# A two-layer attention trunk whose instructions are issued in another written-out order

## The chip, the cores and the metric

The kernel runs on one core of one Trainium2 chip. The metric is the device time of one execution, in microseconds (us). The kernel before took 305.75 us, the median of three runs from 305.56 to 307.73 us. One further execution was taken with the hardware profiler; it took 305.27 us, and 303.5 us of it are the span that the profile shows.

## The reference, cut to what matters

One sequence of 256 tokens with 1024 channels goes through two layers. Each layer computes a shift, a scale and a gate from a condition vector `c`, normalises `x`, projects it, attends and adds the gated result to `x`:

```
cond = silu(c)
for i in range(2):
    shift, scale, gate = split(cond @ ada_w[i] + ada_b[i], 3)
    h = rms_norm(x, norm_g[i]) * (1 + scale) + shift
    y = nsa_mixer(h, ...) if i == 0 else moba_mixer(h, ...)
    x = x + gate * y
```

The first mixer projects `h` to queries, keys and values of three kinds (compressed, selected, window), gates and an output gate `z`. Queries and keys get an RMS norm and a rotation by tables of sines and cosines from the positions. The compressed keys and values go through a small two-layer network. The second mixer is causal attention with 16 heads over 4 key heads. Each mixer ends with a product with an output matrix.

## The kernel before, in words

All weights are read from memory as float32 and split into a high part (rounded to the fast format) and a low part (the rest). Each product is three matmuls: high by high, low by high and high by low. ScalarE makes the high part with a copy, VectorE the low part with a subtraction (`products_of`, lines 1067 and 1068, for the first projection; `parts_of` for later ones).

**The order is written out by hand.** The kernel does not issue instructions where its code stands. It records them as numbered operations with their dependences (`Plan.record`), and at the end `Plan.issue` goes through the list `ORDER`, 2403 numbers, and issues the operations one after the other. Since almost all instructions are issued by one line of `Plan.issue`, they all have line 302 in the profile; groups are told apart by the names of their tiles. The list sets three things. Each engine (TensorE, ScalarE, VectorE, GpSimd and SyncE, which issues most transfers) takes its operations in the order of the list, and waits where an operand isn't ready. A tile gets its buffer when its first operation is issued, from those that earlier tiles have given back. And the transfers get their completion semaphores in that order.

**The opening.** SyncE loads the two halves of `x` (operations 1 and 2) and the weights, stage by stage. ScalarE's queue issues three small transfers: `c` (0), `norm_g` (3) and `ada_b` (4), into the tiles `rot` and `y`. GpSimd's queue issues eight: the norm weights and the gate bias (6 to 10, one row tile `y`), two for the compression (11 and 12, tile `rot`) and the positions (5, tile `rs`). The first projection is done for eight slices of 128 channels, k = 0 to 7. For a slice, four transfers bring the piece of `ada_w` for shift and scale (tile `early`, 41 to 44 for k = 0, 48 to 51 for k = 1), three bring the weight rows (45 to 47 for k = 0). TensorE then runs these steps before the first projection matmul (102):

- 18 to 37: twenty matmuls on an identity that only keep the engine busy.
- 16: transpose of `c`; VectorE and ScalarE make the gated condition `condz` from it (17, 38 to 40).
- 72, 74, 78, 80: transposes of the normalised `x`, four to a group; ScalarE copies the results into `xT` (73, 75, 79, 81).
- 85 and 86 (k = 0), 122 and 123 (k = 1): the condition times `ada_w`, eight calls each, into one row; VectorE copies the row (87, 124).
- 88, 125: a matmul with a selector (`selP`) that turns the row into columns.
- 82: transpose of `norm_g` and `ada_b` into columns (`RT`, 83 and 84). VectorE makes the affine pair `AB` from the columns and 88 (89, 90).
- 91 to 93: ScalarE and VectorE write the slice of `h`, the tile `HT`, high and low part, for k = 0.
- 222, 226, 293: small matmuls that spread the norm weights over all partitions, transpose the positions, and transpose the compression rows.

GpSimd then computes the rotation tables from the positions (228 on). After the eight slices come the key norm and rotation, the compression network, the queries, the blocks of `z`, two pairs of attention heads and the output product, and then the second layer in the same way. While the attention of the first layer runs, side work (the other parts of `ada_w`) is put between.

Of the kernel before, what the change touches and what calls it, by code (L numbers as in the profile page):

```python
# [37 lines left out]
    0, 48, 41, 1, 2, 42, 45, 43, 44, 50, 18, 19, 20, 21, 22, 23, 24, 16, 25, 26, 27, 28, 29, 30, 31, 32, 52, 17, 38,  # L38
    3, 39, 54, 55, 40, 56, 53, 4, 62, 63, 57, 64, 58, 65, 59, 33, 85, 34, 35, 36, 37, 60, 66, 61, 67, 70, 12, 5, 8,
    10, 9, 11, 6, 7, 68, 69, 71, 72, 86, 87, 74, 76, 88, 82, 78, 77, 49, 51, 47, 46, 122, 80, 123, 83, 84, 90, 89,  # L40
    225, 226, 94, 73, 75, 91, 108, 81, 95, 102, 103, 99, 105, 106, 100, 164, 132, 133, 177, 165, 131, 175, 162, 163,
    323, 176, 324, 219, 206, 207, 209, 208, 221, 220, 124, 227, 92, 93, 110, 101, 116, 125, 222, 109, 117, 126, 224,
    127, 223, 79, 128, 148, 104, 118, 107, 113, 114, 111, 115, 112, 119, 150, 120, 121, 293, 156, 153, 134, 129,
    149, 130, 135, 13, 294, 96, 154, 157, 97, 139, 98, 151, 178, 136, 137, 166, 167, 326, 325, 179, 168, 192, 152,
    142, 169, 143, 170, 171, 14, 15, 172, 173, 193, 174, 331, 332, 144, 145, 146, 147, 189, 158, 140, 194, 159, 160,
    138, 161, 200, 201, 202, 186, 180, 181, 141, 203, 190, 191, 295, 296, 228, 271, 229, 230, 231, 232, 270, 272,
    278, 233, 234, 235, 236, 237, 238, 250, 239, 240, 241, 242, 243, 244, 245, 251, 246, 247, 248, 249, 263, 252,
    253, 254, 264, 265, 266, 284, 255, 273, 309, 210, 211, 155, 195, 212, 213, 183, 184, 197, 185, 198, 204, 215,
    214, 216, 187, 188, 306, 182, 205, 196, 303, 311, 300, 297, 310, 317, 298, 318, 333, 217, 334, 218, 329, 327,
    328, 330, 335, 336, 319, 320, 321, 322, 301, 304, 305, 312, 199, 302, 314, 307, 337, 338, 339, 313, 315, 316,  # L50
    299, 308, 349, 351, 350, 380, 411, 412, 381, 414, 382, 413, 416, 415, 418, 599, 417, 439, 437, 352, 366, 353,
    340, 342, 341, 367, 344, 343, 282, 256, 257, 258, 280, 259, 292, 275, 290, 260, 288, 261, 287, 274, 289, 281,
    262, 267, 279, 269, 268, 283, 286, 276, 285, 291, 277, 360, 374, 361, 354, 371, 375, 345, 376, 372, 373, 377,
    355, 368, 346, 383, 362, 391, 356, 369, 378, 397, 357, 370, 358, 419, 347, 420, 384, 402, 421, 422, 423, 348,
    359, 385, 399, 388, 379, 363, 364, 365, 394, 389, 392, 390, 405, 393, 395, 386, 387, 396, 424, 438, 469, 620,
    576, 577, 468, 470, 621, 598, 643, 580, 642, 794, 764, 749, 841, 440, 425, 426, 427, 398, 428, 429, 430, 406,
    403, 404, 407, 400, 408, 409, 410, 431, 445, 448, 442, 401, 441, 454, 432, 455, 433, 462, 449, 451, 443, 578,
    452, 586, 579, 450, 463, 464, 465, 466, 587, 588, 459, 446, 447, 434, 471, 476, 589, 479, 460, 444, 472, 435,
    461, 436, 467, 590, 456, 457, 458, 591, 473, 477, 485, 600, 478, 608, 490, 601, 486, 491, 492, 474, 480, 609,
    610, 453, 482, 481, 483, 644, 507, 510, 511, 622, 623, 592, 593, 594, 595, 596, 597, 614, 615, 616, 617, 618,  # L60
    619, 611, 612, 636, 613, 630, 631, 632, 633, 634, 637, 475, 638, 484, 645, 750, 751, 487, 639, 640, 641, 488,
    665, 635, 655, 656, 666, 667, 489, 668, 669, 670, 842, 508, 843, 509, 503, 765, 501, 502, 504, 500, 505, 506,
    844, 493, 657, 658, 659, 758, 494, 752, 845, 846, 753, 754, 847, 848, 849, 856, 495, 660, 857, 496, 759, 760,
    755, 497, 566, 858, 859, 766, 756, 761, 860, 762, 861, 763, 773, 757, 767, 768, 498, 774, 769, 770, 561, 771,
    520, 521, 672, 522, 779, 602, 871, 901, 512, 872, 874, 671, 780, 523, 524, 525, 662, 526, 527, 781, 673, 873,
    554, 677, 567, 528, 710, 513, 625, 581, 499, 661, 902, 663, 850, 556, 568, 529, 569, 530, 570, 565, 559, 678,
    795, 775, 571, 851, 852, 776, 777, 875, 720, 876, 877, 778, 772, 788, 878, 879, 886, 853, 887, 888, 789, 782,
    790, 572, 574, 903, 783, 854, 855, 889, 890, 791, 891, 792, 904, 905, 906, 862, 863, 793, 864, 865, 804, 796,
    558, 674, 562, 564, 557, 679, 518, 603, 515, 624, 582, 583, 584, 585, 604, 605, 606, 607, 907, 866, 784, 785,
    908, 909, 916, 805, 786, 917, 918, 806, 787, 807, 808, 919, 920, 867, 563, 680, 555, 575, 531, 560, 532, 533,  # L70
    681, 536, 682, 664, 676, 534, 535, 683, 684, 537, 685, 686, 675, 687, 573, 688, 689, 690, 691, 550, 546, 547,
    921, 551, 944, 945, 947, 647, 646, 519, 652, 626, 627, 628, 629, 648, 649, 650, 651, 693, 692, 694, 695, 552,
    553, 946, 538, 702, 548, 703, 549, 542, 543, 797, 708, 544, 696, 653, 869, 868, 709, 948, 949, 809, 798, 950,
    880, 799, 800, 951, 952, 959, 801, 881, 539, 882, 883, 802, 884, 885, 704, 711, 712, 713, 714, 810, 715, 540,
    803, 739, 545, 716, 697, 698, 717, 746, 744, 811, 718, 541, 719, 812, 654, 724, 699, 705, 721, 725, 813, 726,
    814, 727, 815, 728, 870, 899, 928, 516, 929, 1019, 898, 700, 706, 960, 961, 1008, 962, 963, 994, 988, 964, 707,
    816, 729, 817, 730, 818, 731, 819, 723, 722, 820, 732, 745, 747, 821, 733, 1009, 734, 735, 737, 822, 995, 823,
    989, 736, 824, 738, 900, 930, 748, 826, 825, 740, 1079, 517, 1074, 1077, 941, 942, 1010, 1011, 1020, 971, 997,
    992, 701, 991, 993, 996, 931, 990, 1002, 932, 935, 934, 933, 1073, 1076, 514, 1080, 827, 741, 998, 1012, 1124,
    892, 742, 1104, 893, 828, 1003, 835, 829, 999, 1007, 1005, 1001, 743, 1000, 1013, 1125, 972, 1006, 1014, 1105,  # L80
    1114, 1028, 975, 894, 1115, 1126, 1109, 1127, 895, 896, 897, 910, 911, 1021, 1029, 912, 1128, 913, 1030, 1117,
    1004, 1116, 1107, 1015, 1108, 976, 836, 977, 830, 1016, 978, 979, 1017, 936, 1106, 1018, 1129, 980, 938, 939,
    940, 937, 1197, 981, 1195, 1131, 1194, 1196, 943, 1118, 1022, 914, 1110, 915, 1075, 1078, 1081, 831, 1031, 922,
    923, 924, 925, 1023, 926, 927, 953, 954, 1024, 1025, 955, 1032, 1026, 1027, 1034, 1035, 1036, 1037, 956, 1033,
    1040, 957, 958, 965, 1207, 1119, 982, 983, 1111, 1193, 1198, 984, 1120, 1211, 1113, 1130, 1123, 1121, 1112,
    1122, 1209, 1208, 1132, 985, 1134, 1202, 1200, 1201, 1082, 839, 833, 837, 1041, 966, 967, 968, 1042, 1043, 969,
    1044, 970, 1133, 986, 1213, 1199, 1203, 987, 1204, 832, 1210, 834, 840, 1217, 973, 1215, 1216, 1214, 838, 1212,
    1038, 1205, 1206, 974, 1218, 1260, 1233, 1045, 1039, 1219, 1220, 1261, 1091, 1388, 1360, 1162, 1094, 1046, 1047,
    1351, 1350, 1265, 1352, 1263, 1262, 1264, 1163, 1048, 1093, 1135, 1136, 1399, 1361, 1234, 1235, 1353, 1236,
    1223, 1227, 1224, 1230, 1237, 1228, 1222, 1221, 1229, 1055, 1056, 1256, 1049, 1050, 1051, 1052, 1057, 1058,  # L90
    1059, 1060, 1067, 1053, 1054, 1257, 1238, 1061, 1252, 1062, 1063, 1064, 1065, 1270, 1068, 1069, 1277, 1164,
    1253, 1137, 1225, 1231, 1259, 1239, 1398, 1258, 1362, 1254, 1400, 1278, 1281, 1070, 1066, 1138, 1071, 1283,
    1271, 1284, 1139, 1072, 1266, 1363, 1267, 1140, 1141, 1144, 1142, 1143, 1150, 1151, 1145, 1152, 1246, 1279,
    1255, 1282, 1273, 1272, 1280, 1146, 1301, 1153, 1147, 1148, 1149, 1156, 1157, 1287, 1154, 1297, 1285, 1269,
    1247, 1251, 1286, 1240, 1401, 1288, 1298, 1268, 1249, 1250, 1248, 1155, 1291, 1158, 1370, 1165, 1166, 1167,
    1274, 1090, 1389, 1087, 1088, 1290, 1289, 1292, 1299, 1300, 1296, 1275, 1276, 1302, 1241, 1322, 1242, 1226,
# [1399 lines left out]
```

## Time and profile before

| what | value |
| --- | --- |
| median of the runs shown | 305.75 us |
| the profiled execution | 305.27 us, span 303.5 us |
| TensorE busy | 288.7 us |
| VectorE busy | 255.2 us |
| ScalarE busy | 193.6 us |
| GpSimd busy | 45.9 us |
| moved by transfers | 70.83 MB, mean 233 GB/s |

In the profile PE is TensorE, PEld its weight loads, DVE VectorE, ACT ScalarE, POOL GpSimd and SP SyncE; "ACTq" and "SPq" are the issue queues of ScalarE and SyncE. A row of a timeline gives the start, the duration, the engine, the operation with "output <- input" tiles, how many instructions were merged, and in brackets how long the engine had been idle before it and what ended that. In the table by stretches, each engine has its busy time and the number of instructions; PEclk is the granted clock of TensorE as a share of full speed.

### The profile page before, as it was taken

What the parts mean: (1) busy time and instruction counts of PE and PEld (TensorE: products, weight loads), DVE (VectorE), ACT (ScalarE), POOL (GpSimd) and SP (SyncE); (2) the same over time, 40 slices, a digit from 0 to 9 for tenths busy, and PEclk for the clock granted to TensorE, in tenths of its full rate; (3) what the DMA queues carried; (4) which work ended last, traced back from release to release, by engine and by line L of the source; (5) the groups of instructions that cost most, each with busy time, mean ns of one, the idle gap of its engine ahead of it and who ended that gap; (6) DMA issues with size and microseconds to landing.
All of it is one profiled execution on the core that took longest, in us unless ns stands there. A gap on an engine that the chain in (4) does not pass through costs nothing.

```text
span 303.5 us, 6982 instructions
## 1 busy us (share of the span) xinstructions
PE 288.7 (95%) x2612; PEld 242.2 (80%) x2612; DVE 255.2 (84%) x541; ACT 193.6 (64%) x464; POOL 45.9 (15%) x111
## 2 busy tenths in 40 slices
PE   8669999999999899999999999989999999999994
PEld 7547777889886688878997788768887999897874
DVE  0436879976799999998999988996699999999985
ACT  1454434258730768998899926686565899999320
POOL 8503889940000000000000100000000000000000
PEclk9769999999999999999999999999999999999999
DMA  6999999975849999999687959326776994494003
GB/s 197 310 318 337 309 368 362 350 253 172 271 143 298 333 348 368 314 267 277 148 246 229 277 147 350 148 69 208 237 251 186 229 217 131 118 260 145 2 0 138
DMA packets 48698, 70.83 MB, mean 233 GB/s; under 512 B 4919, under 2 KB 24985, under 8 KB 48666
## 3 DMA queue, kind: packets, MB, share of 16 engines
q1 hardware_dynamic: 48298, 70.34, 75.2%
q8 instruction: 20, 0.33, 0.5%
q14 instruction: 12, 0.10, 0.1%
q0 software_dynamic: 256, 0.02, 0.1%
q10 hardware_dynamic: 112, 0.04, 0.1%
HBM read 67.76 MB, written 2.62 MB: 232 GB/s over the span
## 4 chain that ended last, share of the span: by engine, by line
PE 64%; DVE 16%; ACT 8%; DMA 6%; issue 4%; SPq 2%; ACTq 0%; DVEq 0%
PE ps L302 64%; DVE part L302 5%; ACT p L302 3%; DVE buf L302 3%; DMA early<-in_ada_w_dram 3%; ACT part L302 2%; DVE rs L302 2%; DMA buf<-in_moba_w_in_dram 2%; SPq L302 2%; DMA y<-in_ada_b_dram 2%; DVE p L302 1%; DVE ss L302 1%; ACT y L302 1%; ACT buf L302 1%; DVE KTA L302 1%
## 5 line engine op out<-in xcount | busy, mean ns | idle before, releaser
L302 PE MATMUL ps<-part,HT 128*128 128x512 f32 (+2 forms) x408 | 97.2, 376 | 0.3 <-DVE part L302 0.3
L302 PEld LDWEIGHTS ps<-part,HT 128*128 128x128 f32 x408 | 69.0, 189 | 13.4 <-issue 1.0
L302 DVE TENSOR_TENSOR part<-buf,part 128x1024 fp32r<-128x1024 f32 (+2 forms) x58 | 63.7, 1116 | 7.1 <-ACT part L302 6.0
L302 PE MATMUL ps<-HT,part 128*128 128x256 f32 x384 | 66.7, 292 | 0.0
L302 ACT CAST part<-buf 128x1024 fp32r<-128x1024 f32 (+2 forms) x58 | 55.5, 977 | 12.4 <-PE ps L302 6.5
L302 PEld LDWEIGHTS ps<-HT,part 128*128 128x128 f32 x384 | 54.5, 190 | 3.1 <-issue 0.6
L302 PE MATMUL ps<-part,qg 128*128 128x512 f32 (+1 forms) x240 | 48.7, 353 | 0.0
L302 PEld LDWEIGHTS ps<-part,qg 128*128 128x128 f32 x240 | 38.5, 188 | 7.2 <-issue 1.0
L302 ACT ACTIVATE p<-ps,tiny 128x256 f32<-128x256 f32 (+1 forms) x96 | 39.8, 470 | 4.0 <-DVE tiny L302 4.0
L302 PE MATMUL ps<-KTA,qg 128*128 128x256 f32 (+1 forms) x192 | 29.8, 284 | 0.5 <-ACT qg L302 0.5
L302 PEld LDWEIGHTS ps<-KTA,qg 128*128 128x128 f32 x192 | 25.6, 189 | 1.9 <-ACT qg L302 0.7
L302 DVE TENSOR_REDUCE tiny<-ps 128x2 f32<-128x512 f32 (+2 forms) x40 | 23.9, 628 | 1.1 <-PE ps L302 1.0
L302 ACT ACTIVATION_READ_ACCUMULATOR p<-ps,tiny 128x1 f32 x96 | 24.4, 255 | 0.0
L302 ACT ACTIVATE p<-p,tiny 128x256 f32<-128x256 f32 x48 | 22.4, 569 | 0.0
L302 DVE STREAM_TRANSPOSE p<-p 128x1536 f32<-128x1536 f32 x12 | 21.0, 1766 | 0.9 <-ACT p L302 0.4
L302 ACT ACTIVATE HT<-buf,AB 128x256 fp32r<-128x256 f32 x8 | 4.7, 600 | 24.8 <-DVE AB L302 24.8
L302 ACT COPY buf<-ps 128x512 f32<-128x512 f32 (+1 forms) x25 | 11.3, 496 | 12.7 <-PE ps L302 12.2
L302 DVE TENSOR_TENSOR part<-early,part 128x1024 fp32r<-128x1024 f32 (+1 forms) x16 | 17.7, 1108 | 1.2 <-PE ps L302 0.6
L302 ACT CAST part<-early 128x1024 fp32r<-128x1024 f32 (+1 forms) x16 | 14.3, 932 | 1.0 <-DMA early<-in_nsa_w_in_dram 1.0
L302 ACT COPY y<-buf 128x512 f32<-128x512 f32 x6 | 3.6, 617 | 15.2 <-DVE buf L302 15.2
L302 ACT CAST qg<-g 128x512 fp32r<-128x512 f32 x8 | 4.9, 620 | 11.7 <-DVE g L302 11.7
L302 PE MATMUL ps<-buf,condz 128*32 128x256 f32 x192 | 12.0, 382 | 0.0
(191 smaller groups left out, 416.7 us busy)
## 6 DMA issues: line engine op xcount, KB each, us to landing
buf<-in_ada_w_dram SPq DMA_DIRECT2D x32, 512.0 KB, 5.5
buf<-in_moba_w_in_dram SPq DMA_DIRECT2D x20, 512.0 KB, 5.2
early<-in_ada_w_dram SPq DMA_DIRECT2D x32, 256.0 KB, 6.5
buf<-in_nsa_w_in_dram SPq DMA_DIRECT2D x12, 512.0 KB, 5.4
early<-in_nsa_w_in_dram SPq DMA_DIRECT2D x8, 512.0 KB, 5.9
buf<-in_nsa_cmp_w_dram SPq DMA_DIRECT2D x8, 512.0 KB, 6.0
buf<-in_nsa_w_out_dram SPq DMA_DIRECT2D x16, 256.0 KB, 7.8
buf<-in_moba_w_out_dram SPq DMA_DIRECT2D x16, 256.0 KB, 5.2
```

The source lines that it names most:

```text
L302: getattr(self.engines[op["engine"]], method)(*[self._real(a) for a in args], **{k: self._real(a) for k, a in kw.items()})
```

## The change

Only the list `ORDER` changes; the 2403 operations, their tiles and dependences stay the same. The new list differs from the old nearly everywhere. Its beginning, as a diff:

```
 ORDER = [
-    0, 48, 41, 1, 2, 42, 45, 43, 44, 50, 18, 19, 20, 21, 22, 23, 24, 16, 25, 26, 27, 28, 29, 30, 31, 32, 52, 17, 38,
-    3, 39, 54, 55, 40, 56, 53, 4, 62, 63, 57, 64, 58, 65, 59, 33, 85, 34, 35, 36, 37, 60, 66, 61, 67, 70, 12, 5, 8,
-    10, 9, 11, 6, 7, 68, 69, 71, 72, 86, 87, 74, 76, 88, 82, 78, 77, 49, 51, 47, 46, 122, 80, 123, 83, 84, 90, 89,
-    225, 226, 94, 73, 75, 91, 108, 81, 95, 102, 103, 99, 105, 106, 100, 164, 132, 133, 177, 165, 131, 175, 162, 163,
...
+    2, 1, 3, 0, 4, 49, 42, 43, 44, 51, 41, 48, 50, 45, 18, 19, 20, 21, 22, 16, 23, 24, 25, 26, 27, 28, 29, 30, 53,
+    17, 52, 38, 62, 63, 54, 55, 56, 57, 64, 58, 39, 65, 59, 60, 61, 70, 76, 31, 32, 33, 34, 35, 36, 7, 6, 9, 8, 10,
+    12, 11, 5, 66, 40, 67, 68, 37, 72, 85, 86, 122, 69, 77, 87, 123, 78, 88, 82, 83, 84, 124, 90, 89, 73, 71, 74,
+    94, 95, 132, 47, 46, 133, 131, 162, 164, 323, 165, 324, 163, 177, 175, 325, 206, 176, 208, 219, 207, 209, 326,
...
```

The same beginning, queue by queue:

| queue | before | after |
| --- | --- | --- |
| SyncE | 48, 41, 1, 2, 42, 45, 43, 44, 50, 49, 51, 47, 46 | 2, 1, 49, 42, 43, 44, 51, 41, 48, 50, 45, 132, 47, 46 |
| ScalarE | 0, 52, 38, 3, 53, 4, 71, 76, 94, 73, 75, 91 | 3, 0, 4, 53, 52, 38, 76, 73, 71, 94, 75, 91 |
| TensorE, after the twenty | 72, 86, 74, 88, 82, 78, 122, 80, 123, 226, 102 (85 is before the last four of the twenty) | 72, 85, 86, 122, 123, 78, 88, 82, 74, 80, 222, 125, 293, 102 |
| GpSimd | 12, 5, 8, 10, 9, 11, 6, 7, then the tables | 7, 6, 9, 8, 10, 12, 11, 5, then the tables |

Operations 52 and 53 are the sums of squares of the two halves of `x` on ScalarE, 94 the high part of the first weight rows, 132 a piece of the weight rows for k = 1. The copy of the transposed positions (227 on VectorE), which the rotation tables start from, stands behind 174 (the `HT` low part for k = 2) in the new order; before it stood ahead of 92.

Further on, blocks of the same operations are mixed differently. Ahead of the transposes of the first normalised keys (551 and 547) the new TensorE order has thirteen operations of the `z` blocks, the second query product and the transposes that stood behind 547 before, and has moved three behind.

## The prediction on record

> **What bounds the kernel now.** I read the page first, then the busy times by stretch, then the chain of waits, then the timeline of the first 30 us.
>
> ```profile
> span 303.5 us, 6982 instructions
> PE 288.7 (95%) x2612; PEld 242.2 (80%) x2612; DVE 255.2 (84%) x541; ACT 193.6 (64%) x464; POOL 45.9 (15%) x111
> ```
> ```profile
> 0.00:7.60 7.60, 6.16 (x30) 5.92 (x31) 0.17 (x1) 1.28 (x1) 6.23 (x35) 1.00 0.67 198
> 7.60:15.20 7.60, 5.21 (x50) 3.96 (x50) 3.15 (x21) 3.31 (x7) 4.39 (x9) 0.78 1.10 309
> 15.20:22.80 7.60, 4.79 (x47) 3.36 (x47) 2.27 (x7) 4.28 (x8) 0.00 (x0) 0.63 1.00 316
> 22.80:60.70 37.90, 37.87 (x245) 29.62 (x238) 31.91 (x64) 14.45 (x20) 30.31 (x61) 0.98 1.07 345
> 60.70:76.00 15.30, 15.30 (x90) 13.57 (x89) 10.30 (x13) 10.92 (x20) 3.66 (x5) 1.00 0.64 214
> 76.00:100.00 24.00, 21.98 (x148) 18.23 (x147) 21.45 (x60) 9.78 (x18) 0.00 (x0) 1.00 0.78 243
> 100.00:303.50 203.50, 197.38 (x2021) 167.54 (x2018) 185.95 (x379) 149.59 (x396) 1.35 (x2) 1.00 0.69 208
> ```
>
> The columns are the stretch and its length, then the busy time of PE, PEld, DVE, ACT and POOL, the granted clock, the DMA share and GB/s. TensorE is the bound: from 22.8 to 76 us it has no gap (37.87 of 37.90, 15.30 of 15.30). It idles 6.64 us in the first 22.8 us, 2.02 us between 76 and 100 us, and 6.12 us after that. So an order can gain by starting the products earlier, and by filling the later gaps; the same matmuls have to run either way. The chain of waits says what sets the start:
>
> ```profile
> 4.14 1.73 SPq L302
> ...
> 5.92 7.93 DMA early<-in_ada_w_dram
> 13.87 4.75 DMA y<-in_ada_b_dram
> 18.66 28.12 PE ps L302 x206
> ```
>
> The small transfer of `ada_b` (operation 4) is issued only at 13.87 us, because it stands on ScalarE's queue behind the second sum of squares and its issue then waits for an earlier `ada_w` transfer. It arrives 4.75 us later. From there TensorE alone carries the chain. The timeline shows what stands behind it:
>
> ```profile
> 10.06 1.06 ACT L302 ACTIVATE buf<-X 128x1024 f32<-128x1024 f32 x1 [0.43 <-DMA X<-in_x_dram]
> 13.87 0.32 ACTq L302 DMA_DIRECT2D y<-in_ada_b_dram  x1
> 14.11 0.65 PE L302 MATMUL ps<-early,condz 128*32 128x128 f32 x16
> 15.07 0.66 PE L302 MATMUL ps<-identF,buf 128*128 128x128 f32 x4 [0.31 <-ACT buf L302]
> 15.53 1.03 ACT L302 CAST part<-early 128x1024 fp32r<-128x1024 f32 x1
> 18.66 0.37 PE L302 MATMUL ps<-identF,y 64*128 64x64 f32 x1 [2.81 <-DMA y<-in_ada_b_dram]
> 18.96 1.11 PE L302 MATMUL ps<-identF,buf 128*128 128x128 f32 x4
> 19.90 0.60 ACT L302 ACTIVATE HT<-buf,AB 128x256 fp32r<-128x256 f32 x1 [2.37 <-DVE AB L302]
> 20.00 1.08 PE L302 MATMUL ps<-early,condz 128*32 128x128 f32 x16
> 23.07 0.26 PE L302 MATMUL ps<-identF,rs 2*128 2x2 f32 x1
> 23.27 2.55 PE L302 MATMUL ps<-part,HT 128*128 128x512 f32 x9
> 25.66 0.28 PE L302 MATMUL ps<-selP,row 128*128 128x2 f32 x2
> 25.87 0.99 PE L302 MATMUL ps<-y,ones 1*128 1x432 f32 x2
> 29.43 0.25 PE L302 MATMUL ps<-identF,rot 36*128 36x36 f32 x1
> ```
>
> TensorE waits 2.81 us for `ada_b` at 18.66, and the first product (operation 102) starts at 23.27 us.
>
> **The change part by part.** First, `c`, `norm_g` and `ada_b` lead ScalarE's queue, and nothing stands ahead of them. The wait of 2.81 us goes. What is late next is not that transfer but the `ada_w` pieces: the new TensorE queue puts the condition products of both slices (85, 86, 122, 123) ahead of 78, 88, 82, 74 and 80, so the eighth piece has to land before the transposes behind it run.
>
> When does it land? The issue rows give the sizes:
>
> ```profile
> early<-in_ada_w_dram SPq DMA_DIRECT2D x32, 256.0 KB, 6.5
> early<-in_nsa_w_in_dram SPq DMA_DIRECT2D x8, 512.0 KB, 5.9
> X<-in_x_dram SPq DMA_DIRECT2D x4, 512.0 KB
> ```
>
> Two halves of `x` and eight pieces are 3.15 MB. The stretches moved 198 GB/s x 7.6 us = 1.50 MB by 7.6 us, and then 309 GB/s, so 3.15 MB have gone at 7.6 + 1.65/0.309 = 12.9 us. A transfer is seen later than its bytes go: before, `x` with two pieces ahead (1.57 MB) went by 7.8 us and was awaited until 10.06, 2.2 us; the fourth piece, with 2.88 MB, went by 12.1 and its landing ends the chain's step at 13.87, 1.8 us. So the eighth piece is there at 14.7 to 15.1 us. SyncE's queue can add to it: its first transfers again have to land before later ones are issued, and that stall can cost up to the 2 us between the bytes of `x` and their landing. I bound the landing by 14.7 and 17.1 and take 15.1, since SyncE stalled in the same way before (1.73 us on one issue at 4.14).
>
> The Trainium skill (DMA: Bandwidth & Descriptors, Anatomy of one DMA) puts a fixed cost of about 2.0 us on each transfer, mostly the receipt of the last byte; the trace agrees, with 1.8 and 2.2 us.
>
> From there TensorE runs, in its new order, 123, three groups of four transposes, 88, 82, 222, 125 and 293, and then 102. A group of 16 condition matmuls took 0.65 or 1.08 us, a group of four transposes 0.66 or 1.11; I take the means, 0.87 and 0.89. The rest is 0.28 + 0.37 + 0.99 + 0.28 + 0.25 = 2.17. So 102 starts at 15.1 + 0.87 + 2.67 + 2.17 = 20.8 us. With the short rows and 14.7 it is 19.5, with the long ones and 17.1 it is 23.7.
>
> The other legs are shorter. The first weight rows (45) bring the sum to 3.67 MB, gone at 14.6 and seen by 16.8; cast by 17.8 (1.03). ScalarE's copy of the last transposes and `HT` (0.60) follow 74, at about 19.6. `condz` now stands behind both squares, but `x` leads SyncE's queue, so it is due before 12 us, ahead of the pieces that it is multiplied with.
>
> So the products start 23.27 - 20.8 = 2.5 us earlier (bounds 3.8 and -0.4). At that point the new order has also done 222, 125 and 293, which before ran among the products, and has still to do 226: 0.99 + 0.28 + 0.25 - 0.26 = 1.26 us. Together **3.7 us** (5.0 to 0.8), and TensorE, which had no gap up to 76 us, carries it on.
>
> Second, GpSimd. Its eight small transfers stand in another order, and its tables start later, since the copy of the positions now stands behind the third slice on VectorE:
>
> ```profile
> 7.76 0.76 POOL L302 DMA_DIRECT2D rot<-in_nsa_cmp_pe_dram  x1
> 11.52 0.48 POOL L302 DMA_DIRECT2D y<-in_nsa_k_norm_dram  x1
> 23.65 0.32 POOL L302 TENSOR_TENSOR rot<-posf,invf 128x16 f32<-128x16 f32 x1 [11.64 <-DVE posf L302]
> 63.93 0.43 POOL L302 TENSOR_TENSOR TS<-NB,TCS 128x48 f32<-128x48 f32 x1
> ```
> ```profile
> 35.92 0.41 DVE L302 TENSOR_TENSOR HT<-rot,HT 128x256 fp32r<-128x256 f32 x1
> 86.00 0.18 DVE L302 COPY TCc<-NBc 64x48 f32<-64x48 f32 x1
> y<-in_nsa_k_norm_dram POOLq DMA_DIRECT2D x1, 0.8 KB, 5.2
> ```
>
> They would start behind the row of 35.92, some 33 us in the new time, 9 us later than 23.65, and end at about 74 instead of 64.4. The first use that I find stood at 86.00, in the new time about 82. That cover of 8 us makes it cost nothing; without it each microsecond would be one. The compression rows are now the sixth and seventh transfer, issued by 11.5, and with 5.2 us there at 17, before 293 needs them at 20.5.
>
> Third, the rest of the list:
>
> ```profile
> 99.56 0.66 PE L302 MATMUL ps<-identF,y 128*128 128x128 f32 x4 [1.25 <-ACT y L302]
> ```
>
> Ahead of these first transposed keys, which TensorE waited 1.25 us for, its new queue has thirteen more operations and three fewer. At 0.28 us for a wide one (2.55 us for nine in the row of 23.27) and half of that for a narrow one, ten more are 1.4 to 2.8 us of work, enough for the 2.02 us of idle time there. It only counts if VectorE, busy 21.45 of 24.00 us, is not what ends the stretch. Bounds 0 and 2.0; I take 0.5, near the lower end, since VectorE is the nearer row. For the remaining blocks I see no row that favours either list: nothing, with 2.2 us to gain at most (6.12 less the last 3.9 us after the final matmul) and as much to lose:
>
> ```profile
> 299.65 0.43 DVE y L302
> ```
>
> **The sum.** 305.27 - 3.7 - 0.5 = 301.1 us for a profiled execution. That of before was 0.48 us under the median, so the median would be **301.5 us**. Its own range, from the bounds of the front, is 299.7 to 304.4.
>
> **The rivals.**
> *The loads pace it.* Between 22.8 and 60.7 us the DMA share is 1.07 at 345 GB/s; if the transfers are the bound there, an earlier first product only waits later. For it speaks that share; against it, that SyncE waited mostly for free buffers:
>
> ```profile
> SPq L302 <- DVE part L302: 66.2, 25, 7.4
> ```
>
> Then only about 1.0 us stays: 304.8 us.
>
> *TensorE starts its products at a low clock.* The clock was 0.63 in the stretch of the wait, and the same groups took 1.08 and 1.11 us instead of 0.65 and 0.66 there. In the new order TensorE idles ahead of the eighth piece and then runs mainly transposes. With the long rows (0.21 + 0.66 over the means) and the nine products of 2.55 us stretched by the same ratio (1.11/0.66, 1.7 us more), the gain shrinks by 2.6: 304.1 us.
> The Trainium skill (TensorE: Matmul & The Clock Gate, Part 1) says that the clock halves after idling and comes back after about 3.4 us of sustained work; by that figure, as an estimate, up to 1.7 us would be lost. The trace's 0.63 fits a mix of both states.
>
> *The small GpSimd transfers hold TensorE: slower than before.* 222 and 293 now stand ahead of every product. If the rows of 293 land as late as the trace allows (it shows only that they were there at 29.43), the first product starts at 29.43 + 0.25 = 29.7 us, 6.4 us late, less the 1.26 already done: 310.9 us. It decides from a landing at 24.3 us on (23.27 + 1.26 - 0.25). Against it stand the 5.2 us to landing.
>
> *All of it comes.* The short rows at the start (5.0) and the filled gap (2.0): 305.75 - 7.0 = 298.7 us.
>
> *The change doesn't do what it says.* `ada_b` may be early and something else just as late, the ninth transfer's stall above all; that is the upper end of the front (0.8 us gained), about 305 us, and I count it with the loads.
>
> **How the numbers follow.** Forecast 0.48, loads 0.20, clock 0.14, slower 0.10, all of it 0.08. The likeliest gives 301.5 us. The range goes from 298.5, just under the last rival, to 306.5, above the loads and the front's upper end; it leaves out most of the slower case. Faster by over 1%, under 302.7 us: most of the forecast (0.44), the last rival (0.08) and a part of the clock (0.03), 0.55. Slower by over 1%: 0.10 and a little of the remaining lists' risk, 0.12. Within 1%: 0.33. One per cent is about what a measurement of this kernel can tell from no change.
>
> **What would show it right or wrong.** Right: `ada_b` is issued in the first 3 us, no TensorE wait names it, the first product matmul (part, HT) starts at 19.5 to 22 us, TensorE idles under 4.5 us in the first 22.8 us and has no gap up to 70 us, and the gap around 95 us is smaller. Wrong: a wait of TensorE for `early` beyond 17 us, for the tiles `y` or `rot` after it, gaps between 23 and 70 us that a weight transfer ends, or a first product as late as 23 us.

## The result and the profile after

The changed kernel took 298.11 us (median of four runs, 297.67 to 298.75); the kernel before, beside it, 305.96 us. The ratio is 0.9738, with a 95% interval from 0.9701 to 0.9775: faster by 2.6%. Timed twice more beside the experiments it gave 0.9805 [0.9734, 0.9876] and 0.9811 [0.9775, 0.9848], so the gain is some 2 to 2.6%. The forecast of 301.5 us was 3.4 us too high, and the time is just under the range. Times below are medians of the executions that no longer stretch of low clock disturbed.

The page of the profile after:

```profile
span 296.3 us, 6988 instructions
PE 286.2 (97%) x2612; PEld 240.8 (81%) x2612; DVE 255.2 (86%) x541; ACT 194.6 (66%) x464; POOL 43.8 (15%) x111
```

Its busy times by the same stretches as before (PE, PEld, DVE, ACT, POOL, then granted clock, DMA share, GB/s):

```profile
0.00:7.60 7.60, 5.29 (x23) 4.98 (x24) 0.79 (x6) 3.68 (x6) 6.23 (x35) 1.00 0.75 238
7.60:15.20 7.60, 7.07 (x98) 6.31 (x98) 3.42 (x19) 2.36 (x4) 4.39 (x9) 1.00 1.16 320
15.20:22.80 7.60, 7.60 (x38) 5.82 (x37) 6.54 (x17) 5.78 (x9) 0.00 (x0) 1.00 1.13 334
22.80:60.70 37.90, 37.61 (x244) 30.05 (x243) 31.97 (x58) 16.13 (x22) 28.22 (x51) 1.00 1.07 354
60.70:76.00 15.30, 15.30 (x108) 14.53 (x107) 9.61 (x15) 12.36 (x20) 3.58 (x15) 1.00 0.94 286
76.00:100.00 24.00, 22.47 (x152) 16.81 (x150) 22.39 (x60) 9.43 (x17) 0.40 (x1) 1.00 0.80 275
```

Three things differ in the opening. TensorE idles 2.84 us in the first 22.8 us instead of 6.64. Its granted clock is 1.00 where it was 0.78 and 0.63. And the transfers move 238 GB/s in the first 7.6 us instead of 198. The timeline after shows the steps (all of it has line 303 now, since the list has one line more):

```profile
1.85 0.33 ACTq L303 DMA_DIRECT2D y<-in_ada_b_dram  x1
4.58 1.06 ACT L303 ACTIVATE buf<-X 128x1024 f32<-128x1024 f32 x1 [1.09 <-DMA X<-in_x_dram]
11.69 2.29 PE L303 MATMUL ps<-early,condz 128*32 128x128 f32 x64 [0.40 <-DMA early<-in_ada_w_dram]
13.34 0.38 PEld L303 LDWEIGHTS ps<-early,condz 128*32 128x32 f32 x16 [0.40 <-DMA early<-in_ada_w_dram]
13.92 0.66 PE L303 MATMUL ps<-identF,buf 128*128 128x128 f32 x4
14.41 0.28 PE L303 MATMUL ps<-selP,row 128*128 128x2 f32 x2
14.62 0.27 PE L303 MATMUL ps<-identF,y 64*128 64x64 f32 x1
14.83 1.09 PE L303 MATMUL ps<-identF,buf 128*128 128x128 f32 x8
15.85 0.99 PE L303 MATMUL ps<-y,ones 1*128 1x432 f32 x2
17.08 0.25 PE L303 MATMUL ps<-identF,rot 36*128 36x36 f32 x1
17.26 0.97 PE L303 MATMUL ps<-part,HT 128*128 128x512 f32 x3
26.00 1.05 ACT L303 CAST part<-early 128x1024 fp32r<-128x1024 f32 x1 [4.48 <-DMA early<-in_nsa_w_in_dram]
84.94 1.39 PE L303 MATMUL ps<-buf,p 128*64 128x256 f32 x8 [1.32 <-DVE p L303]
```

`ada_b` is issued at 1.85 us and no matmul waits for it. The eighth `ada_w` piece is there at 13.34 us, and the first product (102) starts at 17.26 us, 6.01 us earlier than the 23.27 of before, with 1.26 us of other work already done: 7.27 us ahead. At the end the span is 7.2 us shorter. So the whole gain stands at the first product, and the 280 us after it bring nothing in sum.

The low clock of before is sharper in two finer stretches of its own trace:

```profile
10.34:13.63 3.29, 3.29 (x25) 2.65 (x25) 2.14 (x14) 0.87 (x2) 1.67 (x4) 0.50 1.16 292
17.43:24.00 6.57, 5.34 (x44) 3.63 (x45) 2.66 (x9) 2.49 (x5) 0.32 (x1) 0.50 1.00 315
```

TensorE ran at half clock all through both. Read in steps of 0.1 us, the half clock lasts a little longer than these two rows, from 10.32 to 13.74 and from 17.15 to 23.98 us: 3.41 and 6.83 us. Of the second, the 4.61 us from the arrival of `ada_b` at 18.66 us to 23.27 us were work on the way to the first product.

### The profile page after: what moved, and what is told of

It is laid out like the page before. It is cut to its first block, busy times and chain, and to the rows that moved or that the text cites. A ratio compares the mean times of both kernels' runs of the same rounds, so it can differ in the third digit from the quotient of the medians.

```text
span 296.3 us, 6988 instructions
## 1 busy us (share of the span) xinstructions
PE 286.2 (97%) x2612; PEld 240.8 (81%) x2612; DVE 255.2 (86%) x541; ACT 194.6 (66%) x464; POOL 43.8 (15%) x111
## 5 line engine op out<-in xcount | busy, mean ns | idle before, releaser
L303 PE MATMUL ps<-part,HT 128*128 128x512 f32 (+2 forms) x408 | 96.2, 375 | 0.3
L303 PE MATMUL ps<-HT,part 128*128 128x256 f32 x384 | 62.8, 289 | 0.0
L303 PEld LDWEIGHTS ps<-HT,part 128*128 128x128 f32 x384 | 52.8, 189 | 2.9 <-issue 0.9
L303 ACT CAST part<-early 128x1024 fp32r<-128x1024 f32 (+1 forms) x16 | 15.0, 938 | 21.5 <-DMA early<-in_nsa_w_in_dram 21.4
L303 DVE TENSOR_REDUCE tiny<-ps 128x2 f32<-128x512 f32 (+2 forms) x40 | 24.8, 628 | 1.2 <-PE ps L303 1.0
L303 ACT ACTIVATION_READ_ACCUMULATOR p<-ps,tiny 128x1 f32 x96 | 23.4, 244 | 0.0
L303 ACT ACTIVATE p<-p,tiny 128x256 f32<-128x256 f32 x48 | 21.8, 585 | 0.1
L303 PE MATMUL ps<-buf,condz 128*32 128x256 f32 x192 | 11.8, 382 | 0.0
L303 DVE SCALAR_TENSOR_TENSOR sum<-early,condz,sum 128x512 f32<-128x512 f32 x14 | 10.6, 756 | 0.2
L303 POOL MEMSET buf<- 128x1024 f32 x1 | 1.0, 953 | 64.4 <-PE ps L303 64.4
L303 POOL TENSOR_SCALAR rot<-rot 128x16 f32<-128x16 f32 x19 | 10.1, 532 | 1.6
```

What stands on the lines that cost most here:

```text
L303: getattr(self.engines[op["engine"]], method)(*[self._real(a) for a in args], **{k: self._real(a) for k, a in kw.items()})
```

## The experiments

All of them reorder the list or change the number of idle matmuls (18 to 37), whose result nobody reads; where their number changes, that is all that is left out or added. **The theory** is that the opening brings the gain: `ada_b` early, `x` first, and no half clock. **The rival** is that the rest of the new list brings part of it.

**Opening and rest, crossed.** The changed opening with the old rest, and the old opening with the new rest; the seam is operation 102 (two operations of each stand a little later than their list has them, until a buffer is free):

```diff
 new_front_old_rest
-    222, 125, 293, 102, 105, 99, 106, 92,
+    222, 125, 293, 102, 225, 226, 108, 81,
 old_front_new_rest
-    81, 95, 102, 103, 99, 105,
+    81, 95, 102, 124, 132, 133,
```

> The changed list up to and with operation 102 (the first product), then everything that is left in the old list's order. Theory (the whole gain arises ahead of the first product): 298 to 299.5 us, the first product at 17.3 us as in the changed kernel. Rival (the rest of the new list brings part of it, some 2 us or more): 300.5 to 302 us with the same first product.

> The old list up to and with operation 102, then everything that is left in the new list's order. Theory (the rest of the list brings nothing): 304.5 to 306.5 us, first product at 23.3 us. Rival (it brings 2 us or more): under 304 us.

Measured: 302.19 us, ratio 0.9917 [0.9875, 0.9960], first product at 17.40 us; and 305.54 us, ratio 0.9995 [0.9954, 1.0036], first product at 22.14 us (in a profiled execution that took 309.15 us). The second agrees with the theory. The first does not, and comes out just above where the rival had it: the same opening lost over 3 us behind the old rest. A row of its trace shows one such loss, a wait of TensorE for a later piece of `ada_w` that neither the kernel before nor the changed kernel has:

```profile
168.16 1.06 PE L297 MATMUL ps<-buf,condz 128*32 128x256 f32 x12 [1.36 <-DMA buf<-in_ada_w_dram]
```

Its clock was also 0.50 from 18.15 to 21.56 us. So the new rest brings nothing by itself, but it keeps what its opening brings.

**One move at a time.** The three small transfers first, `x` first, and both, with every other queue in the old order:

```diff
 old_small_first
-    0, 48, 41, 1, 2, 42, 45,
+    0, 3, 4, 48, 41, 1, 2, 42, 45,
 old_x_first
+    2, 1, 0, 48, 41, 42, 45,
 old_x_and_small_first, x_small_again
+    2, 1, 3, 0, 4, 48, 41, 42, 45,
```

> The old list, but with the three small transfers 0, 3 and 4 (c, norm_g, ada_b) at the head of ScalarE's queue. Theory (the wait for ada_b is only one part, and the ada_w pieces are late next): TensorE's wait of 2.81 us at operation 82 goes, the first product starts at 20 to 21 us, 302.5 to 303.5 us in all. Rival 1 (the low clock came from that wait alone, so all of it comes): under 301 us. Rival 2 (x or a piece is as late, and the wait only changes its name): over 304.5 us.

> The old list with both halves of x at the head of SyncE's queue and nothing else moved; ada_b stays behind the second sum of squares on ScalarE's queue. Theory (x comes 3.8 to 4 us earlier, so ScalarE reaches the issue of ada_b earlier, but the issue still waits for an earlier transfer): ada_b issued at 6 to 11 us, first product at 18 to 21 us, 300 to 303.5 us. Rival (the wait for a free semaphore holds it as before): ada_b issued at 13 to 14 us, first product at 22.5 to 23.5 us, 304.5 to 306 us.

> The old list, but with both halves of x at the head of SyncE's queue and 0, 3 and 4 at the head of ScalarE's; every compute engine keeps the old order. Theory (the transfers carry most of the gain, TensorE's new order the rest): 300 to 301.5 us, first product at 18.5 to 20 us. Rival 1 (the order on the compute engines brings more than half): 302 to 303.5 us. Rival 2 (the transfers bring all of it): 298 to 299 us.

> The same kernel as old_x_and_small_first, timed in more rounds, since its four runs lay between 298.8 and 305.6 us. Theory 1 (those two moves of transfers are all that the change brings; every other reordering brings nothing): median 298 to 299.5 us. Theory 2 (the rest of the new list keeps about 2 us of it, because behind an earlier front the old list's later transfers arrive late): 300 to 302 us.

Measured: small first 300.24 us, 0.9837 [0.9795, 0.9879]; `x` first 304.22 us, 0.9997 [0.9958, 1.0035]; both 298.80 and 302.10 us at first, and in more rounds 298.69 us, 0.9780 [0.9741, 0.9818], first product at 15.95 and 16.13 us. That last is the changed kernel's own time: two moves of five transfers bring all of it. They bring it less steadily: all ten executions of this kernel lie between 298.06 and 305.59 us, the fourteen of the changed kernel between 297.35 and 300.41; why was not tested. The small transfers alone bring more than the theory's 302.5 to 303.5 us, as the first rival had it (under 301), since both the wait and the half clock behind it go (another stretch of half clock, from 11.3 to 14.7 us, is there in this execution):

```profile
15.46 0.27 PE L297 MATMUL ps<-identF,y 64*128 64x64 f32 x1
15.66 0.66 PE L297 MATMUL ps<-identF,buf 128*128 128x128 f32 x4
18.13 2.11 PE L297 MATMUL ps<-part,HT 128*128 128x512 f32 x8
```

The transposes take 0.66 us, and the first product starts at 18.13 us, ahead of the 20 to 21 expected. With `x` alone, the time lies between what theory and rival had. `ada_b` is issued at 12.00 us, held until an `ada_w` piece has landed at 11.98, and TensorE waits as long as before:

```profile
17.12 0.27 PE L297 MATMUL ps<-identF,y 64*128 64x64 f32 x1 [3.15 <-DMA y<-in_ada_b_dram]
18.54 1.11 PE L297 MATMUL ps<-identF,buf 128*128 128x128 f32 x4
```

The first product starts at 20.79 us, 2.5 us earlier than before, and the time does not follow; where this kernel loses that again, the runs do not show. What `x` first does to the transfers shows in the first 7.6 us of three kernels. Small first alone, with two pieces ahead of `x`:

```profile
0.00:7.60 7.60, 5.62 (x33) 5.28 (x33) 0.17 (x1) 1.28 (x1) 6.23 (x35) 1.00 0.61 194
```

`x` first alone:

```profile
0.00:7.60 7.60, 5.71 (x33) 5.28 (x33) 0.40 (x3) 2.53 (x4) 6.23 (x35) 1.00 0.75 245
```

Both:

```profile
0.00:7.60 7.60, 6.17 (x30) 5.92 (x31) 0.35 (x3) 2.74 (x5) 6.23 (x35) 1.00 0.76 237
```

With `x` in front the rate is 237 to 245 GB/s, else 194 (198 before).

**One move taken back.** The changed list with `ada_b` behind the second sum of squares, and with `x` behind two pieces:

```diff
 new_ada_b_late
-    2, 1, 3, 0, 4, 49, 42,
+    2, 1, 3, 0, 49, 42,
...
-    17, 52, 38, 62, 63,
+    17, 52, 38, 4, 62, 63,
 new_x_late
-    2, 1, 3, 0, 4, 49, 42, 43,
+    3, 0, 4, 49, 42, 2, 1, 43,
```

> The changed list with the transfer of ada_b (4) put back behind the second sum of squares (38) on ScalarE's queue, where the old list has it. Theory (its issue waits for the transfer that stood eight places ahead, now an early one, and it is there before the eighth ada_w piece): issued at 8 to 10 us, no wait of TensorE for it over 0.5 us, first product at 17.2 to 18 us, 297.5 to 299.5 us. Rival (a late issue always costs its full wait): issued at 11 us or later, first product at 19 us or later, 300 to 302.5 us.

> The changed list with the two halves of x put behind the first two ada_w pieces on SyncE's queue, as in the old list. Theory (x first is the other half of the gain: everything up to the first product hangs on the squares of x, and the transfers run slower in the first 7.6 us without it): x seen at 8 to 10 us, under 210 GB/s in the first 7.6 us, first product at 19 to 21 us, 300 to 302 us. Rival (the eighth ada_w piece sets the first product, and it doesn't care which transfer is first): first product at 17 to 18 us, 297.5 to 299.5 us.

Measured: 299.06 us, 0.9792 [0.9739, 0.9845], first product at 17.59 us; and 300.77 us, 0.9843 [0.9801, 0.9885], first product at 20.71 us. Both as the theory had it. With `ada_b` back in its old place:

```profile
8.05 0.32 ACTq L297 DMA_DIRECT2D y<-in_ada_b_dram  x1
14.96 0.27 PE L297 MATMUL ps<-identF,y 64*128 64x64 f32 x1
```

It is issued at 8.05 us, not at 13.87, and nobody waits. Its place on ScalarE's queue did not cost the 2.81 us by itself; the hold of its issue did, which ended with the landing of an `ada_w` piece in both kernels with the old order (at 13.85 us before, at 11.98 with `x` alone in front). With `x` late the transposes come late instead, and the clock falls again behind the wait (0.82 in the stretch from 15.2 us):

```profile
13.32 0.63 PE L297 MATMUL ps<-identF,buf 128*128 128x128 f32 x4 [3.89 <-DVE rs L297]
16.82 1.12 PE L297 MATMUL ps<-identF,buf 128*128 128x128 f32 x4
```

**The half clock by itself.** The old list with six more idle matmuls in the wait for `ada_b` (numbers from 38 up rise by six), and the changed list with five and with twelve idle matmuls instead of twenty:

```diff
 old_spins_in_wait
-    SPINS = 20
+    SPINS = 26
-    80, 82, 94, 88, 84,
+    80, 82, 94, 38, 39, 40, 41, 42, 43, 88, 84,
 new_five_spins
-    SPINS = 20
+    SPINS = 5
 new_12_spins
-    SPINS = 20
+    SPINS = 12
```

> The old list with six more of the idle 128 x 128 matmuls, which nobody reads, put on TensorE's queue just ahead of operation 82, where it waits 2.81 us for ada_b; ada_b comes as late as before. Theory (the granted clock of 0.50 from 17.4 to 24.0 us comes from that wait, and it costs beside the wait): the clock is 1.00 there, the work from 18.7 us to the first product takes 2.0 to 2.8 us instead of 4.6, first product at 20.7 to 21.5 us, 302.5 to 304 us in all. Rival 1 (VectorE and ScalarE set the pace between the arrival and the first product, or the low clock has another cause): first product at 23 us or later, 305 to 306.5 us. Rival 2 (the added matmuls only delay the queue): over 306 us.

> The new list with only the first five of the twenty idle matmuls, so that TensorE has almost nothing to do from 3.5 to 10.7 us; the fifteen that are left out are read by nobody. Theory (an idle TensorE is followed by a stretch of half clock, and the twenty matmuls keep that away in the changed kernel): clock about 0.5 for 3 us or more somewhere between 10 and 17 us, first product at 18.3 to 20 us, 299.2 to 301 us in all. Rival (only the transfers set the first product): first product at 17.0 to 17.5 us, 297.5 to 299 us.

> The changed kernel with twelve idle matmuls instead of twenty, so TensorE is idle for some 1.7 us more before 10.7 us. Theory (shift of the code): waits for issue on TensorE other than 0.2 us, between 0.4 and 4.5 us, and a time longer by their sum. Rival (transfers): 0.2 to 0.4 us. In both the first product is at 17.3 to 18.3 us, and stretches of half clock are more frequent than in the changed kernel, under 1.5 us in the mean.

Measured: old with six more 301.88 us, 0.9902 [0.9866, 0.9939]; changed with five 306.05 us, 1.0068 [1.0017, 1.0118]; with twelve 305.00 us, 0.9967 [0.9919, 1.0014]. In the first, `ada_b` comes as late as before, yet:

```profile
18.85 0.27 PE L298 MATMUL ps<-identF,y 64*128 64x64 f32 x1 [1.07 <-DMA y<-in_ada_b_dram]
19.05 0.66 PE L298 MATMUL ps<-identF,buf 128*128 128x128 f32 x4
21.52 2.22 PE L298 MATMUL ps<-part,HT 128*128 128x512 f32 x9
```

From the arrival to the first product it is 2.67 us instead of 4.61, as expected by the theory, at a clock of 1.00; the whole is a little better than its 302.5 to 304 us. Filling the wait with useless work made the kernel 1% faster. The 1.94 us are the difference of two profiled executions, and chance has a share in where half clock falls: the first stretch of before, at 10.32 us, is gone here too, although nothing was added ahead of it and TensorE waited 3.04 us there instead of 2.08.

The two kernels with fewer idle matmuls took longer than any expectation. Their openings lose under 1 us (first products at 18.20 and 18.11 us). The view prints a clock of 1.00 there, but these traces hold no record of the clock ahead of 14.3 us, and the rows behind the wait of 4.68 us in the kernel with five are long until then and short from there on:

```profile
9.66 1.09 PE L296 MATMUL ps<-identF,buf 128*128 128x128 f32 x4 [4.68 <-DVE rs L296]
14.86 0.66 PE L296 MATMUL ps<-identF,buf 128*128 128x128 f32 x4
```

The changed kernel took 0.60 us for the first of these groups. So, by the rows, TensorE was slow up to about 14.3 us, much as the theory had it, and the first product is 0.94 us later than in the changed kernel. Most of the time went at 137 us. With five:

```profile
141.26 3.58 PE L296 MATMUL ps<-KTA,qg 128*128 128x32 f32 x16 [4.20 <-issue]
```

And the stretch behind that wait:

```profile
141.30:149.00 7.70, 7.70 (x48) 7.38 (x47) 4.33 (x8) 2.95 (x9) 0.00 (x0) 0.60 0.66 158
```

With twelve:

```profile
138.77 0.45 PE L297 MATMUL ps<-p,vr 32*64 32x128 f32 x9 [2.67 <-issue]
```

```profile
138.80:145.00 6.20, 6.20 (x41) 5.82 (x41) 2.76 (x6) 1.00 (x6) 0.00 (x0) 0.64 0.78 177
```

TensorE waited 4.20 and 2.67 us for nothing that the profile shows (printed as a wait for issue), and then ran at a clock of 0.60 and 0.64: with five 4.20 us and 0.40 of 7.70, 7.3 us in all. The same wait is 0.42 us before and 0.15 to 0.44 us in three profiled executions of the changed kernel. With twelve, the wait and the first product came as the theory had them, but the time of 305.00 us is about 4 us more than that wait accounts for.

**The rest of the doubts.** The changed kernel again, twice; five more idle matmuls ahead of operation 85; nineteen idle matmuls; and the two moves as the opening with the new rest behind it:

```diff
 new_25_spins
-    SPINS = 20
+    SPINS = 25
 new_19_spins
-    SPINS = 20
+    SPINS = 19
 two_moves_new_rest
-    2, 1, 3, 0, 4, 49, 42, 43,
+    2, 1, 3, 0, 4, 48, 41, 42,
...
+    81, 95, 102, 124, 132, 133,
```

> The changed kernel itself, so that it is timed beside the others on one chip. Every theory: 297.5 to 299 us, first product at 17.3 us.

> The changed kernel again, for a comparison on the same chip: 297.5 to 299 us by every theory.

> The changed list with five more idle matmuls put ahead of operation 85, where TensorE waits 0.4 to 1.3 us for the ada_w pieces. Theory (gaps of TensorE near the start bring on stretches of half clock by chance, so fewer gaps give fewer of them): mean granted clock 0.999 to 1.000 in nearly all runs, median 297 to 298.2 us. Rival (no gain: the stretches come by themselves, or the added matmuls delay the condition products): 298.3 to 299.5 us.

> The changed kernel with nineteen idle matmuls instead of twenty. Theory (what the runs lose as waits for issue, 0.2 us in the changed kernel and 0.4 to 4.2 us in the others, hangs on where in the instruction stream a 16 KB load of code falls, and any kernel that shifts it changes it): the sum of those waits on TensorE differs from 0.2 us by up to 4 us with all else equal, 297.5 to 302 us. Rival (those waits come from what the transfers do at 135 to 145 us, which this leaves as it is): 0.2 to 0.4 us, 297.5 to 299 us.

> The opening of the kernel with only x and the three small transfers moved to the front (up to and with operation 102), then everything that is left in the new list's order: the earliest first product seen so far with the other list behind it. Theory (the opening sets the gain, the rest of either list keeps it): 297.5 to 299.5 us, first product at 16 us, level with the changed kernel. Rival 1 (an opening and a rest that were not ordered for each other lose 2 us or more): 300 to 302 us. Rival 2 (it beats the changed kernel): under 297 us.

Measured: the changed kernel 298.52 and 298.63 us; the first of these two profiled executions has half clock from 18.0 to 21.4 us all the same, the second has none. Twenty-five idle matmuls 300.04 us, 0.9814 [0.9782, 0.9847]: the clock stayed at 0.998 or above, as the theory had it, but the first product slipped to 18.08 us and the waits for issue grew to 2.1 us, so there is no gain, and the time is above even the rival's. Nineteen 298.25 us, 0.9788 [0.9751, 0.9825], with the wait for issue still at 0.2 us, as the rival (the transfers) had it; with twelve the rival missed. Nor does a shift of TensorE's instructions have to be there: the kernel with the two moves has the twenty idle matmuls and the TensorE order of before, and its waits for issue were 1.60 and 2.01 us in two executions, against 0.42. So neither account holds for all kernels, and no row shows what the engine waits for. The two moves with the new rest 301.52 us, 0.9895 [0.9856, 0.9935], though the first product starts at 15.96 us, as early as in the kernel with the two moves:

```profile
17.05 0.96 PE L297 MATMUL ps<-y,ones 1*128 1x432 f32 x2 [0.59 <-DMA y<-in_nsa_k_norm_dram]
32.65 2.82 PE L297 MATMUL ps<-part,HT 128*128 128x512 f32 x13 [1.07 <-ACT HT L297]
```

New waits stand behind the seam, and the clock fell to 0.87 between 20 and 27 us. An early opening with the other list's rest took about 302 us both times, with its own rest 298.1 to 298.7. None of the kernels beat the changed one.

## Why the prediction was wrong

The direction and the path to the first product were right; two terms of the sum were too large, the second in half because it counted rows of a half clock that went away with the wait. Point by point:

**The wait for `ada_b` goes, and the `ada_w` pieces are late next.** Right: no wait names `ada_b`, and TensorE's weight loads stood 0.40 us for the eighth piece.

**The eighth piece is there at 15.1 us (14.7 to 17.1).** This step failed: 13.34 us. I carried the 198 GB/s of before over to a list that issues `x` first. With the measured 238, 1.81 MB are moved by 7.6 us, and 1.34 MB at 320 GB/s take 4.2 us more: the bytes are gone at 11.8 and not at 12.9, which is 1.1 us of the 1.8. The other 0.7 us are the landing delay: I took 2.2 us, the larger of my two, and it was 1.5. The Trainium skill (DMA: Bandwidth & Descriptors, Anatomy of one DMA) puts it at about 2.0 us, for transfers issued from GpSimd; these came from SyncE. The kernels with one move show that `x` first made the rate: 245 against 194.

**From there 5.7 us to the first product.** This failed too: 13.34 to 17.26 is 3.92 us. I took the mean of short and long rows, 0.66 and 1.11 us for four transposes. The long rows were no spread: those of before lie in its stretch of half clock, 17.15 to 23.98 us. The short rows alone give 0.65 + 3 x 0.66 + 2.17 = 4.80; the other 0.9 us is that a row's end lies behind the start of the next (two groups in one row, 1.09 us). The two steps are 1.8 + 1.8 us: all of the 3.5 us between 20.8 and 17.26. The miss of 3.4 us is nearly the same, because two smaller errors cancel: the 0.5 us for the rest of the list did not come, and the 0.48 us by which the median lay above the profiled execution were gone after the change (298.11 and 298.08). The sum's own range also has a slip: its lower end leaves these 0.48 us out and should read 300.2.

**The rival of a low clock** had the thing the wrong way round. I asked whether the new order would keep the low clock of 0.63, and not what the old order paid for it. The six idle matmuls put a price on it: 1.94 us between the arrival and the first product. The Trainium skill (TensorE: Matmul & The Clock Gate, Part 1) has a free-running window of about 3.4 us and a clock that falls to one half after an idle one. The trace agrees on the half and on the length (3.41 and 6.83 us), but the stretches came with waits of only 2.1 and 2.8 us, the second beginning inside its wait, and none came behind the 3.04 us in the old list with six more idle matmuls. So the length of a wait alone does not tell whether half clock follows. Over the executions compared, the mean clock was 0.980 to 0.994 before, and 0.991 to 1.000 in the changed kernel.

**GpSimd costs nothing.** Right: the transposes of `rot` and the products with `y` at 15.85 and 17.08 us waited for nothing, so that rival is out. The tables started late, at 29.37 us instead of 23.65, and no wait of TensorE names them.

**The rest of the list: 0.5 us.** Roughly right in its place and nothing on balance: the two waits of 0.78 and 1.25 us became 1.32 and 0.21 us, and TensorE idles 0.49 us less between 76 and 100 us, but 0.26 us more between 22.8 and 60.7.

**The rival of the loads** holds for ScalarE, which waits 4.48 us for weights ahead of 26.00 us, and not for TensorE. **All of it comes** (298.7 us) was nearest to the time, though from the opening and not from the filled gap.

Open: what the waits for issue wait for. With the changed list they are 0.15 to 0.44 us with twenty idle matmuls, 0.2 with nineteen, 2.1 with twenty-five, 2.67 with twelve and 4.20 with five; with the two moves on the old list 1.60 and 2.01. The cause was not shown. Open too: what decides whether a wait is followed by half clock.

## What to carry to other kernels

A duration from a stretch of low granted clock may be part of the price of the wait ahead of it: when a change takes the wait away, also work out the time with the rows behind it at full clock. Before you trust a printed clock, compare the length of the same rows elsewhere. Look for the few small transfers at the head of the kernel that everything hangs on, and put them first; here five moves out of 2403 brought the time of the whole new list, if less steadily. Treat an opening and the rest of a written-out order as one schedule, since an early opening before the other list's rest lost 3 us, twice.

## What was not expected of the hardware

- In the profiled executions a wait of TensorE cost more than itself: 2.81 us of wait and 1.94 us of half clock after it. Idle matmuls that filled the wait won 1%.
- Removing matmuls that nobody reads made the kernel slower by 7 us: a wait of 4.20 us for nothing that the profile shows came up 130 us later, and a clock of 0.60 behind it. Why is open.
- The same transfers in another order moved 194 or 245 GB/s in the first 7.6 us.
